# Low parts of the input projections' weights made by an adding DMA

## The chip, the cores and the metric

The kernel runs on one core of one Trainium2 chip. A core has a matrix engine (TensorE, PE in the profile, with its weight loads listed as PEld), three engines for elementwise work (VectorE = DVE, ScalarE = ACT, GpSimd = POOL) and SyncE (SP), which here only issues DMAs. SP, ACT and POOL can issue DMAs; all of them run on the core's 16 DMA engines. The engines work through their own queues of instructions in order, and wait for one another by semaphores. The metric is the device time of one execution in microseconds, the median of several runs.

## The reference

One decoder layer for two groups of tokens with shared weights: a prompt of 1024 positions, and 8 decoding requests of 8 positions (64 in all). The model is 1024 wide.

```python
xn = rmsnorm(x, norm1_g)
proj = xn @ w_in                       # 1024 x 5632: q, k, v, glu_a, glu_b, gate_a, gate_b
q, k, v, glu_a, glu_b, gate_a, gate_b = jnp.split(proj, SPLIT_IDX, axis=-1)
attn = ...                             # sliding window of 128, with sinks
branch_a = attn @ w_o_attn
u = glu_a * jax.nn.sigmoid(glu_b)
c = dwconv_valid(u_ext, conv_b_w, conv_b_bias)      # causal, 31 taps
branch_b = jax.nn.silu(layernorm(c, ln_b_g, ln_b_b)) @ w_pb
merged = jax.nn.sigmoid(gate_a) * branch_a + jax.nn.sigmoid(gate_b) * branch_b
h = x + merged @ w_out
...                                    # a feed-forward block with a short convolution, final norm
```

All tensors are float32. What the edit touches is `w_in`, the weight of the first product.

## The kernel before

**Products in three parts.** TensorE is used with the type float32r, which keeps fewer bits than float32. To keep float32's accuracy, each operand is split in a high part, the value rounded to float32r, and a low part, what the rounding left off. Each product is then three matmuls added up in PSUM (`mm3`, L177 to L181): high weight by high activation (L179), high weight by low activation (L180), low weight by high activation (L181). L181 is the only one that reads a weight's low part as its stationary operand; the two value weights are used the other way round, as moving operands.

**Weights.** All 134 weight tiles lie in one DRAM array `wall`, each 128 partitions by 1024 floats (512 KB), in the order in which they are used (`weight_order`). The first 44 belong to the input projections; `n_in` is 44. `w_load` (L138 to L143) has SP load tile `i` into `wraw`, which has two buffers. `w_split` (L145 to L159) makes the two parts: ScalarE copies the raw tile to `whi` with rounding (L157), VectorE subtracts the rounded tile from the raw one and writes `wlo` (L158). There are two pairs of `whi` and `wlo`, taken in turn, with a tile of the attention pool for one value weight.

**Streams.** `stream` (L183) takes one weight tile and runs it over all 1088 tokens, in chunks of 384, 384 and 320 columns, with 8 slices of 128 rows each: 24 groups of three matmuls. `weight` (L167) is called at the head of each stream and splits the next tile, too: so while stream `i` runs, the parts of tile `i+1` are made, into the pair that stream `i-1` has just let go.

**What runs beside it.** The order of the input streams is written out by hand (`SEQUENCE`). The first four weights run in a stage of their own with the first norm. Then, for each of the eight channel blocks, a `b` and an `a` stream give `u`; `a_done` (L585) has POOL store the convolution's state (`o_cbp`, L587, and `o_cbs`, L588, whose rows are runs of 30 floats) and puts the convolution (`conv`, L405) behind by 1200 steps of priority. The convolution is mostly VectorE's (L417), and its result overwrites `u` and is stored by POOL in two DMAs (`d_c`, L440 and L441). POOL also sets the margins of the next `u` to zero (L558, L559), for which it waits until the stores have read that buffer. Gate streams store their result by POOL (L611), and spills of the attention's output go by POOL, too (L340, L341). Attention units are handed out in small steps between the groups of the streams (`tick`), in two stretches.

The order of the instructions of each engine is set when the kernel is built: among those that are ready by the builder's own simulated time, the one with the best priority goes first. On the chip each engine keeps that order.

Of the kernel before, what the change touches and what calls it, by code (L numbers as in the profile page):

```python
# [6 lines left out]
F32 = mybir.dt.float32  # L7
F32R = mybir.dt.float32r
AF = mybir.ActivationFunctionType
ALU = mybir.AluOpType  # L10
# [35 lines left out]
FIRST = 4  # L46
# [69 lines left out]
class Build:  # L116
# [28 lines left out]
    def w_split(self):  # L145
        i = len(self.w_hl)
        if i < len(self.order):
            r = self.w_raw[i]
            pool, x = self.slot(i)
            th, tl = x if isinstance(x, tuple) else (f"whi{x}", f"wlo{x}")  # L150
            n = 2 if th == tl else 1
            h = self.t(pool, [P, DM], th, F32R, bufs=n)
            l = self.t(pool, [P, DM], tl, F32R, bufs=n)
            m = W_PARTS if i < FIRST else 1
            for x in range(m):
                z = slice(x * DM // m, (x + 1) * DM // m)
                self.nc.scalar.copy(h[:, z], r[:, z])  # L157
                self.nc.vector.tensor_tensor(l[:, z], r[:, z], h[:, z].bitcast(F32), ALU.subtract)  # L158
            self.w_hl.append((h, l))  # L159
# [1216 lines left out]
```

## Time and profile before

| what | value |
|---|---|
| median of 3 runs | 1712.88 us (1711.49 to 1713.6) |
| profiled execution, its own time | 1713.01 us |
| span of the profiled execution | 1711.2 us |
| mean clock granted to TensorE | 0.993 |
| matmul instructions | 11390, busy 98% of the span |
| VectorE, ScalarE, GpSimd busy | 75%, 49%, 14% |

A line of the profile that names a group reads: code line, engine, operation, tile written <- tiles read, shape, count, then busy time and the mean of one in ns, and then how long the engine stood idle just before these instructions and which engine, tile and line ended most of that. A line of a timeline begins with its start and its length in us. The lines of DMA issues give the kilobytes of one and the median time from issue to landing in us. Matmuls overlap in the array, so the listed length of one (about 330 ns) is more than the distance from one to the next.

### The profile page before, as it was taken

Reading aid. Unit: us, or ns where it says so; the run is one execution under the profiler, and the core shown is the slowest. Engines: PE = TensorE matmul, PEld = TensorE weight load, DVE = VectorE, ACT = ScalarE, POOL = GpSimd, SP = SyncE. Lnnn points to the kernel's source line nnn. Section 1 sums busy time; section 2 is a strip of 40 time slices with the busy share of each in tenths; the row PEclk is TensorE's granted clock in tenths of the full one; section 3 lists DMA queues with packets and bytes.
Section 4 is the critical chain, followed back from the end, with each engine's and each line's share of the span. In section 5 each row is a group of like instructions: output and inputs, shape, how many; then the busy total and the mean of one; then the engine's idle time right before and its main releaser. Section 6 shows DMA issues by size and latency. Waiting matters only on the chain.

```text
span 1711.2 us, 29156 instructions
## 1 busy us (share of the span) xinstructions
PE 1681.5 (98%) x11390; PEld 1659.8 (97%) x11390; DVE 1290.3 (75%) x2236; ACT 847.1 (49%) x1718; POOL 242.0 (14%) x430
## 2 busy tenths in 40 slices
PE   9999999999999999999999999999999997999998
PEld 8899999999999999999999999999999996999997
DVE  8999989999579986755447968777777775654437
ACT  7524577733588737963224535444444445211102
POOL 1300112130011111100000432222222210000000
PEclk9999999999999999999999999999999998999999
DMA  5112223232211274544344232222222217643102
GB/s 195 51 53 74 67 63 97 78 125 61 76 44 56 75 259 150 171 159 138 115 132 131 71 110 65 76 77 77 77 77 79 80 62 228 195 121 102 52 1 105
DMA packets 103466, 172.16 MB, mean 101 GB/s; under 512 B 44400, under 2 KB 69376, under 8 KB 103312
## 3 DMA queue, kind: packets, MB, share of 16 engines
q1 hardware_dynamic: 89760, 124.92, 24.2%
q0 software_dynamic: 13424, 45.15, 7.2%
q8 instruction: 89, 1.46, 0.4%
q14 instruction: 49, 0.40, 0.1%
q10 hardware_dynamic: 144, 0.23, 0.0%
HBM read 124.74 MB, written 47.50 MB: 101 GB/s over the span
## 4 chain that ended last, share of the span: by engine, by line
PE 86%; DVE 10%; ACT 2%; DMA 1%; issue 1%; SPq 0%; DVEq 0%; ACTq 0%
PE mm L179 21%; PE mm L180 21%; PE mm L181 21%; PE aux L181 6%; PE aux L180 6%; PE aux L179 6%; DVE c L417 3%; PE aux L303 1%; DVE bt L417 1%; PE aux L315 1%; PE aux L316 1%; PE aux L293 1%; DVE wlo L158 1%; PE aux L294 1%; DVE q L627 1%
## 5 line engine op out<-in xcount | busy, mean ns | idle before, releaser
L179 PE MATMUL mm<-xh,whi 128*128 128x384 f32 (+1 forms) x944 | 314.6, 333 | 0.4 <-ACT xh L217 0.4
L180 PE MATMUL mm<-xl,whi 128*128 128x384 f32 (+1 forms) x944 | 309.2, 328 | 2.5 <-DVE xl L245 1.5
L181 PE MATMUL mm<-xh,wlo 128*128 128x384 f32 (+1 forms) x944 | 308.8, 327 | 0.0
L157 ACT CAST whi<-wraw 128x1024 fp32r<-128x1024 f32 (+1 forms) x91 | 93.6, 1031 | 193.7 <-PE aux L180 104.3
L180 PEld LDWEIGHTS mm<-xl,whi 128*128 128x128 f32 x944 | 177.9, 188 | 5.4 <-DVE xl L245 2.3
L179 PEld LDWEIGHTS mm<-xh,whi 128*128 128x128 f32 x944 | 178.0, 189 | 1.6 <-ACT xh L217 0.7
L181 PEld LDWEIGHTS mm<-xh,wlo 128*128 128x128 f32 x944 | 177.7, 188 | 0.1
L158 DVE TENSOR_TENSOR wlo<-wraw,whi 128x1024 fp32r<-128x1024 f32 (+1 forms) x91 | 108.6, 1197 | 23.5 <-ACT whi L157 23.2
L997 DVE SCALAR_TENSOR_TENSOR acc<-st,fc,acc 128x1104 f32<-128x1104 f32 x88 | 119.8, 1363 | 3.2 <-ACT acc L995 2.5
L179 PE MATMUL mm<-mh,whi 128*128 128x272 f32 x400 | 115.9, 290 | 0.0
L180 PE MATMUL mm<-ml,whi 128*128 128x272 f32 x400 | 115.3, 288 | 0.0
L181 PE MATMUL mm<-mh,wlo 128*128 128x272 f32 x392 | 113.4, 289 | 0.0
L179 PE MATMUL mm<-gh,whi 128*128 128x384 f32 (+3 forms) x264 | 86.4, 327 | 12.5 <-ACT gh L196 12.5
L417 DVE SCALAR_TENSOR_TENSOR bt<-u,consts,bt 128x513 f32<-128x513 f32 x120 | 89.8, 748 | 0.6
L417 DVE SCALAR_TENSOR_TENSOR c<-sm,hsum,c 128x512 f32<-128x512 f32 x120 | 89.6, 746 | 0.7
L181 PE MATMUL mm<-gh,wlo 128*128 128x384 f32 (+3 forms) x264 | 86.5, 328 | 0.0
L179 PE MATMUL aux<-gh,whi 128*128 128x384 f32 (+3 forms) x264 | 86.3, 327 | 0.0
L180 PE MATMUL mm<-gll,whi 128*128 128x384 f32 (+3 forms) x264 | 86.3, 327 | 0.0
L181 PE MATMUL aux<-gh,wlo 128*128 128x384 f32 (+3 forms) x264 | 86.1, 326 | 0.0
L180 PE MATMUL aux<-gll,whi 128*128 128x384 f32 (+3 forms) x264 | 86.0, 326 | 0.0
L417 DVE SCALAR_TENSOR_TENSOR c<-u,consts,c 128x512 f32<-128x512 f32 x112 | 83.5, 746 | 0.4
L180 PEld LDWEIGHTS mm<-ml,whi 128*128 128x128 f32 x400 | 75.4, 188 | 0.0
(362 smaller groups left out, 5166.5 us busy)
## 6 DMA issues: line engine op xcount, KB each, us to landing
wraw<-wall SPq DMA_DIRECT2D x134, 512.0 KB, 3.9
d_g<-acc POOLq DMA_DIRECT2D x22, 552.0 KB, 5.0
gr<-d_g SPq DMA_DIRECT2D x22, 512.0 KB, 5.0
ga<-d_ga SPq DMA_DIRECT2D x8, 544.0 KB, 4.1
gb<-d_gb SPq DMA_DIRECT2D x8, 544.0 KB, 3.6
mar<-d_ma SPq DMA_DIRECT2D x8, 544.0 KB, 5.5
xr<-xT SPq DMA_DIRECT2D x32, 136.0 KB, 2.6
d_h<-H POOLq DMA_DIRECT2D x4, 1088.0 KB, 5.8
```

The costliest lines, as they stand in the source:

```text
L157: self.nc.scalar.copy(h[:, z], r[:, z])
L158: self.nc.vector.tensor_tensor(l[:, z], r[:, z], h[:, z].bitcast(F32), ALU.subtract)
L179: mm(ps, wh, xh, start=first, stop=False, skip_group_check=more)
L180: mm(ps, wh, xl, start=False, stop=False, skip_group_check=more)
L181: mm(ps, wl, xh, start=False, stop=last, skip_group_check=more)
L293: nc.tensor.matmul(ps[:, j, :], q[g][:, h, qs], kd[g][:, keys], start=True, stop=False)
L294: nc.tensor.matmul(ps[:, j, :], q[g][:, h, qs], kl[g][:, keys], start=False, stop=True)
L303: nc.tensor.transpose(ps[:, h * P:(h + 1) * P], pt[:, h, kb * P:(kb + 1) * P], self.ident)
L315: nc.tensor.matmul(av, v, ph, start=kb == kbs[0], stop=False)
L316: nc.tensor.matmul(av, v, pl, start=False, stop=kb == kbs[-1])
L417: mac = lambda o, x, w: nc.vector.scalar_tensor_tensor(o, x, w, o, ALU.mult, ALU.add)
L997: nc.vector.scalar_tensor_tensor(acc, st[:, k:k + AW], fw(f, k), acc, ALU.mult, ALU.add)
```

## The change

For the tiles 4 to 43 of `wall` (`FIRST <= i < n_in`: the input projections' weights, but for the first four) the low part is made in another way. ScalarE makes the rounded tile as before, then reads it back and writes its negative to the tile of the low part. GpSimd then issues a DMA from the raw weight in DRAM to that tile with the operation "add": what lies there, minus the rounded weight, is replaced by its sum with the raw weight. VectorE has no part in it. The raw tile in SBUF is still loaded, and read by the rounding copy alone.

```diff
@@ -151,6 +151,12 @@
             n = 2 if th == tl else 1
             h = self.t(pool, [P, DM], th, F32R, bufs=n)
             l = self.t(pool, [P, DM], tl, F32R, bufs=n)
+            if FIRST <= i < self.n_in:
+                self.nc.scalar.copy(h, r)
+                self.nc.scalar.activation(l, h.bitcast(F32), AF.Identity, scale=-1.0)
+                self.nc.gpsimd.dma_start(l, self.a["wall"][i], accum_op=ALU.add)
+                self.w_hl.append((h, l))
+                return
             m = W_PARTS if i < FIRST else 1
             for x in range(m):
                 z = slice(x * DM // m, (x + 1) * DM // m)
```

All other weights, and the splitting of the activations, stay as they were.

## The prediction

> **What bounds the kernel now.** I read the page's busy table and its chain first, then stage windows of the input projections, then the PE's waits there.
>
> ```profile
> span 1711.2 us, 29156 instructions
> PE 1681.5 (98%) x11390; PEld 1659.8 (97%) x11390; DVE 1290.3 (75%) x2236; ACT 847.1 (49%) x1718; POOL 242.0 (14%) x430
> PE 86%; DVE 10%; ACT 2%; DMA 1%; issue 1%; SPq 0%; DVEq 0%; ACTq 0%
> L181 PE MATMUL mm<-xh,wlo 128*128 128x384 f32 (+1 forms) x944 | 308.8, 327 | 0.0
> ```
>
> The whole span has 30 us without a matmul (1711.2 - 1681.5). L181 is the only matmul that reads the low part as a stationary operand, and its 944 instructions waited 0.0 us. The low part is therefore never late today.
>
> ```profile
> 79.00:110.00 31.00, 31.00 (x187) 31.00 (x188) 30.68 (x45) 10.28 (x19) 4.44 (x8) 1.00 0.26 67
> 110.00:200.00 90.00, 89.71 (x609) 88.92 (x608) 88.69 (x149) 37.26 (x87) 7.90 (x16) 1.00 0.21 62
> 200.00:350.00 150.00, 148.29 (x959) 143.07 (x958) 139.50 (x317) 115.66 (x290) 30.00 (x62) 1.00 0.25 79
> 350.00:455.00 105.00, 105.00 (x643) 104.96 (x642) 94.62 (x143) 36.95 (x73) 17.04 (x34) 1.00 0.30 94
> 455.00:600.00 145.00, 143.99 (x941) 139.38 (x940) 124.48 (x305) 122.15 (x316) 20.71 (x42) 1.00 0.18 56
> 600.00:640.00 40.00, 40.00 (x245) 39.79 (x244) 33.62 (x52) 14.50 (x24) 6.49 (x12) 1.00 0.75 264
> PE aux L315 <- ACT pth L196: 1.7, 2, 1.0
> PE aux L316 <- DVE ptl L197: 0.9, 1, 0.9
> PE mm L180 <- POOL xl L245: 0.6, 1, 0.6
> ```
>
> The columns are stage, length, then PE, PEld, DVE, ACT and POOL busy, the clock, the DMA share and GB/s. In the stage the edit touches, VectorE is busy for 511.6 of 561 us and looks like the bound. PE has only 561 - 558.0 = 3.0 us of gaps, at clock 1.00, and VectorE ended 0.9 us of PE's waits. So 3.0 us is all the stage can give.
>
> **The change part by part.** Forty of the 44 input weights change (44 less FIRST = 4).
>
> ```profile
> L158 DVE TENSOR_TENSOR wlo<-wraw,whi x38: 1210/1220/1230, 82.7 to 637.9; 128x1024 fp32r<-128x1024 f32 x38
> L157 ACT CAST whi<-wraw 128x1024 fp32r<-128x1024 f32 x38 | 40.0, 1053 | 46.9 <-PE mm L180 46.0 <-ACT u L572 0.2
> L577 ACT ACTIVATE u<-u 128x1024 f32<-128x1024 f32 x7 | 7.4, 1064 | 0.1
> L611 POOL DMA_DIRECT2D d_ga<-gt x21 | 11.4, 545 | 50.7 <-ACT gt L608 48.4 <-PE aux L303 1.7 <-ACT av L369 0.6
> ```
>
> *Removed:* 40 subtractions of 1.22 us, 48.8 us of VectorE. They lie beside matmuls, so they are worth at most the 0.9 us of PE's wait on VectorE: I take -0.9.
>
> *Added on ScalarE:* 40 activations, priced by the same-shape ACTIVATE at 1.06 us: 42.6 us, one behind each rounding copy. In the plain stages (37.26 of 90 busy) they hide. In the two attention stages ScalarE stands at 237.8 of 295 us. Some 17 weights fall there, 18 us more, 81% to 87%. It ended 1.7 us of PE's waits on pth; bounds 0 and a doubling, and I take +1.5 because the load is already high. PSUM evacuations and exponentials queue behind each activation.
>
> *Added on GpSimd:* 40 issues; the 545 ns row makes 22 us on an engine busy 86.6 of 561. Hidden as time. The gate stores behind them have no reader before the output projection.
>
> *Moved:* the raw tile is released by the rounding copy instead of the subtraction, so SyncE's next 512 KB load starts a few us sooner, beside the adding DMA. Loads are not late now; the cost falls on the adding DMA. HBM reads grow by 40 x 0.5 MB at a DMA share near 0.2; hidden.
>
> **The new chain.** What matters is the time from a stream's start (when its predecessor's tiles come free) to the next stream's first L181.
>
> ```profile
> 102.96 0.34 PE L179 MATMUL mm<-xh,whi 128*128 128x384 f32 x1
> 114.82 0.34 PE L179 MATMUL mm<-xh,whi 128*128 128x384 f32 x1
> 115.17 0.35 PE L181 MATMUL mm<-xh,wlo 128*128 128x384 f32 x1
> 383.80 1.05 ACT L157 CAST whi<-wraw 128x1024 fp32r<-128x1024 f32 x1 [7.90 <-PE mm L180]
> 395.96 0.35 PE L181 MATMUL mm<-xh,wlo 128*128 128x384 f32 x1
> ```
>
> From 102.96 to 115.17 there are 12.2 us. Rounding copy and activation take 0.05 + 1.05 + 1.06 = 2.2; I add 0.3 for GpSimd to come round to it, an estimate of half an issue. That leaves 9.7 us for the adding DMA, issue to landing. In the attention stages 295 us for some 17 weights is 17.4 each, so about 5 us more.
>
> ```profile
> wraw<-wall SPq DMA_DIRECT2D x39, 512.0 KB, 3.5
> d_c<-u POOLq DMA_DIRECT2D x8, 512.0 KB, 2.9
> o_cbs<-u POOLq DMA_DIRECT2D x8, 120.0 KB, 6.5
> ```
>
> No row shows an adding DMA. A plain load of the size lands in 3.5 us, a plain store in 2.9. The adding one reads raw weight and destination and writes. Lower bound: a plain load, 3.5. Upper: twice a load then a store, 12.8. I take one load and one store end to end, 6.4, nearest in bytes. With 6.4 against 9.7, most of the 40 hide with 3.3 us to spare.
>
> By the Trainium skill, "Collectives: The Full Stack", section "The bandwidth ceiling" (the addition in the DMA engine costs no time of its own; the second source that is read halves the rate), this DMA would land only a little after a load, an estimate; the time would then be that of the rival below in which everything hides. No run here shows an adding DMA yet.
>
> **What comes late.** The spare is used up where GpSimd's queue holds something slow ahead of the adding DMA.
>
> ```profile
> 129.92 0.56 POOL L441 DMA_DIRECT2D d_c<-u  x1 [22.88 <-DVE u L436]
> 133.44 0.54 POOL L440 DMA_DIRECT2D d_c<-u  x1 [2.96 <-DVE u L438]
> 137.16 0.12 POOL L558 MEMSET u<- 128x30 f32 x1 [3.19 <-DMA d_c<-u]
> ...
> 386.56 0.86 POOL L588 DMA_DIRECT2D o_cbs<-u  x1 [0.58 <-issue]
> 387.33 0.62 POOL L440 DMA_DIRECT2D d_c<-u  x1
> 394.83 0.12 POOL L558 MEMSET u<- 128x30 f32 x1 [6.87 <-DMA d_c<-u]
> ```
>
> The store at 133.44 landed 3.7 us later (the memset waits for it). The same store at 387.33, right behind o_cbs with its 120-byte pieces (30 floats each, by the code), landed 7.5 us later. So what follows o_cbs on GpSimd's DMA queue is 3.8 us late. An adding DMA there needs 6.4 + 3.8 = 10.2, and is issued only at 387.4: it lands at 397.6 against 395.96, a stall of 1.6. o_cbs follows each a stream; the plain ones are those after 102.96 and 383.75 (the others have attention's spare): 2 x 1.6 = 3.2 us.
>
> Around 130 the queue waits for the convolution on VectorE (22.88 us) and for its landing.
>
> ```profile
> 127.83 1.05 ACT L157 CAST whi<-wraw 128x1024 fp32r<-128x1024 f32 x1
> 138.89 0.35 PE L181 MATMUL mm<-xh,wlo 128*128 128x384 f32 x1
> 142.47 1.03 ACT L157 CAST whi<-wraw 128x1024 fp32r<-128x1024 f32 x1
> ```
>
> Here the low part is ready to add at 127.83 + 2.11 = 129.9. Ahead of L441 it costs nothing; behind the memset, issue at 137.3 and landing at 143.7, 4.8 us late; behind L440, 140.4, late by 1.5. I take the middle one, 1.5. The copy at 142.47 is 3.9 us into its stream: 144.6 + 6.4 = 151.0 against 150.75 (138.89 and 11.86): 0.3.
>
> **Sum:** -0.9 + 1.5 + 3.2 + 1.5 + 0.3 = +5.6 us, against the profiled run's 1713.0 (the span and 1.8 us around it; 0.1 above the median of 1712.9): 1718.6. The collisions' order on GpSimd can't be read from this trace, and a load beside each adding DMA makes 6.4 optimistic by up to its own 3.5; one us on those five late places adds 4, so I set the forecast at **1720**, own range 1716.5 to 1735.
>
> **Rivals.** *The adding DMA itself is too slow.* From 9.7 us up, each plain stream stalls by the excess. The plain streams show by the copy that starts with each, first and last of a stretch:
>
> ```profile
> 91.15 1.06 ACT L157 CAST whi<-wraw 128x1024 fp32r<-128x1024 f32 x1 [0.44 <-PE mm L180]
> 360.10 1.06 ACT L157 CAST whi<-wraw 128x1024 fp32r<-128x1024 f32 x1 [2.28 <-PE mm L180]
> 431.28 1.05 ACT L157 CAST whi<-wraw 128x1024 fp32r<-128x1024 f32 x1 [2.93 <-PE mm L180]
> 613.13 1.06 ACT L157 CAST whi<-wraw 128x1024 fp32r<-128x1024 f32 x1 [2.32 <-PE mm L180]
> 636.82 1.05 ACT L157 CAST whi<-wraw 128x1024 fp32r<-128x1024 f32 x1 [2.84 <-PE mm L180]
> ```
>
> Seven from 360.10 to 431.28 at 11.86 apiece, three from 613.13 on, and seven from 79 to 162 (one copy ahead of 91.15): 17. At the upper bound of 12.8 that is 17 x 3.1 = 53, and with the forecast's 5.6 on top 1713.0 + 58.6, near 1772. For: no row prices it, and it reads three streams' worth beside a load. Against: 6.4 by the nearest rows. *Everything hides:* landing under 5 us, or GpSimd's queue kept in readiness order. L181 is never late, 1712 to 1714; this is the other side, and the point is an o_cbs-delayed landing below 8.6 us (395.96 - 387.4). For: 12.2 us a stream and a GpSimd idle 85%. *VectorE's relief shows:* the convolutions end sooner, evacuations and splits too, and all 3.0 us of gaps go: 1709 to 1710. Against: VectorE ended 0.9 us of waits only. *The change doesn't relieve anything:* the freed VectorE only idles; that is the second rival's time.
>
> The Trainium skill, "DMA: Bandwidth & Descriptors", Queues, rings and completion order, has each DMA engine consume a ring's descriptors in order, and its section "SWDGE vs HWDGE vs iDMA" gives GpSimd one queue. By that rule the o_cbs wait is real, and the late store at 387.33 agrees (7.5 us against 3.7).
>
> **How the numbers follow.** Forecast 0.36; too slow a DMA 0.32; all hidden 0.22; relief shows 0.10. About 0.2% (3.4 us) is what a measurement can tell from no change. The first two are slower, 0.68; same 0.22; faster 0.10. The range goes down to 1709.5 for most of the relief, and up to 1785 for the slow DMA with the forecast's terms and a little above its bound; the forecast's own range stands above.
>
> **What would show it.** Right: L181 of the changed weights with waits on the DMA of wlo, single digits of them, after o_cbs and after convolution stores; adding DMAs of 5 to 9 us; VectorE some 49 us lighter, ScalarE 43 us heavier; PE's busy sum unchanged. Wrong upward: nearly every plain stream begins with a stall of one size, and landings above 9.7 us. Wrong downward: L181 still at 0.0, landings below 5 us. Also wrong: new PE waits on ScalarE's p or pth of more than 5 us, which would put the cost on the activation.

## The result and the profile after

| | before | changed |
|---|---|---|
| median of 17 runs | 1713.38 us | 1716.53 us |
| ratio, 95% interval | | 1.0018 [1.0011, 1.0025] |
| profiled execution, its span | 1713.01, 1711.2 us | 1715.69, 1713.9 us |

The change costs 3.1 us of 1713 (the profiled pair: 2.7). The interval leaves out 1, so the kernel became slower. The cost is about half of the forecast's 7 and just under the bound of 0.2% that was set for "no change", and 1716.53 lies at the very bottom of the forecast's own range, 1716.5 to 1735. In the changed file the lines after the edit stand six further down: L181 is now L187, L303 is L309, L441 is L447.

The page of the changed kernel, the lines that answer to those of before:

```profile
span 1713.9 us, 29215 instructions
PE 1682.1 (98%) x11390; PEld 1659.5 (97%) x11390; DVE 1245.4 (73%) x2196; ACT 884.3 (52%) x1758; POOL 283.6 (17%) x470
L187 PE MATMUL mm<-xh,wlo 128*128 128x384 f32 (+1 forms) x944 | 309.0, 327 | 3.3 <-DMA wlo<-wall 3.3
wlo<-wall POOLq DMA_DIRECT2D x39, 512.0 KB, 6.6
```

VectorE is 45 us lighter and ScalarE 37 us heavier. PE's busy sum moved by 0.6 us. The adding DMA lands in 6.6 us at the median; the forecast took 6.4. L187 now waits, 3.3 us in all. The stages, in the windows view of the changed kernel, with the same columns as before:

```profile
60.00:79.00 19.00, 17.20 (x103) 16.58 (x102) 18.21 (x29) 12.00 (x25) 9.94 (x13) 1.00 0.27 63
110.00:200.00 90.00, 88.21 (x597) 86.92 (x595) 88.50 (x153) 45.89 (x97) 15.11 (x26) 1.00 0.47 107
200.00:350.00 150.00, 149.29 (x956) 144.64 (x957) 124.57 (x299) 122.90 (x295) 37.64 (x68) 0.99 0.43 109
350.00:455.00 105.00, 103.74 (x634) 103.38 (x632) 77.40 (x123) 43.13 (x78) 31.47 (x42) 1.00 0.59 135
455.00:600.00 145.00, 144.04 (x932) 137.88 (x931) 121.03 (x305) 127.91 (x319) 27.09 (x50) 1.00 0.37 85
```

PE's waits in the changed kernel between 60 and 645 us (sum in us, count, longest):

```profile
PE mm L187 <- DMA wlo<-wall: 3.3, 3, 1.8
PE aux L322 <- DVE ptl L203: 1.6, 2, 1.5
PE aux L321 <- ACT pth L202: 1.5, 5, 0.6
```

The row of before for the first of these stages, which the forecast did not look at:

```profile
60.00:79.00 19.00, 16.94 (x89) 15.41 (x88) 18.88 (x28) 10.06 (x21) 7.95 (x8) 0.91 0.25 82
```

The three waits of the changed kernel's L187, in its PE timeline:

```profile
64.69 0.45 PE L187 MATMUL mm<-xh,wlo 128*128 128x384 f32 x1 [1.79 <-DMA wlo<-wall]
112.70 0.44 PE L187 MATMUL mm<-xh,wlo 128*128 128x384 f32 x1 [0.25 <-DMA wlo<-wall]
443.82 0.44 PE L187 MATMUL mm<-xh,wlo 128*128 128x384 f32 x1 [1.26 <-DMA wlo<-wall]
```

**Where the time went.** A sum of waits doesn't show this well. What does is the start of each stream (its first high-by-high matmul), compared kernel by kernel. Rows of before and of the changed kernel between which the lead changes:

```profile
62.89 0.34 PE L179 MATMUL mm<-xh,whi 128*128 128x384 f32 x1
79.26 0.34 PE L179 MATMUL mm<-xh,whi 128*128 128x384 f32 x1
455.84 0.34 PE L179 MATMUL mm<-xh,whi 128*128 128x384 f32 x1
599.38 0.34 PE L179 MATMUL mm<-xh,whi 128*128 128x384 f32 x1
```

```profile
62.38 0.34 PE L185 MATMUL mm<-xh,whi 128*128 128x384 f32 x1
76.36 0.34 PE L185 MATMUL mm<-xh,whi 128*128 128x384 f32 x1
456.37 0.34 PE L185 MATMUL mm<-xh,whi 128*128 128x384 f32 x1
601.54 0.34 PE L185 MATMUL mm<-xh,whi 128*128 128x384 f32 x1
```

The same subtraction (start in the named kernel less start in before, us) for the changed kernel and for six of the experiments below; the stream itself is named by its start in before. A number that falls from one row to the next is a gain in between, one that rises a loss:

| start in before | what lies ahead of it | changed | first_two | first_two_b | plain_only | act_only | dma_only | plain_copy |
|---|---|---|---|---|---|---|---|---|
| 62.89 | | -0.5 | +1.3 | -0.4 | -0.5 | +1.2 | -0.2 | -0.5 |
| 79.26 | first stage's end | -2.9 | -1.2 | -2.8 | -2.9 | +1.5 | +4.8 | -2.9 |
| 188.71 | plain streams | -2.4 | -1.2 | -2.8 | -2.5 | +2.6 | +5.5 | -2.9 |
| 207.57 | attention, its first stream | -1.3 | +0.4 | -2.8 | -2.8 | +1.6 | +3.8 | -1.1 |
| 360.05 | attention, the rest | -1.0 | +0.3 | -2.8 | -2.7 | +2.3 | +3.7 | -0.8 |
| 455.84 | plain streams | +0.5 | +0.3 | -2.8 | -1.6 | +2.3 | +3.7 | -0.8 |
| 599.38 | attention | +2.2 | +0.3 | -2.8 | -1.6 | +3.4 | +3.6 | +0.8 |
| 648.63 | plain streams | +2.2 | +0.3 | -2.8 | -1.6 | +3.4 | +4.4 | +0.9 |

The changed kernel gains 2.4 us in the first stage, loses 0.5 and 1.5 in plain streams, and 1.4 and 1.6 beside attention. The gain takes back about half of three kinds of loss.

A trace is one execution, and a dip of TensorE's clock can sit in any of its rows. `first_two` and `first_two_b` are the same kernel. The first had lost 1.6 us more at 62.89, with a granted clock of 0.91 over its first 20 us against 1.00 in before, and it loses 1.6 us from 188.71 to 207.57, where its clock reads 0.83. So a step of one or two us in a single trace proves little by itself; what several traces agree on does more.

### The profile page after: what moved, and what is told of

Its sections match the earlier page's. It is cut to its first block, busy times and chain, and to the rows that moved or that the text cites. A ratio compares the mean times of both kernels' runs of the same rounds, so it can differ in the third digit from the quotient of the medians.

```text
span 1713.9 us, 29215 instructions
## 1 busy us (share of the span) xinstructions
PE 1682.1 (98%) x11390; PEld 1659.5 (97%) x11390; DVE 1245.4 (73%) x2196; ACT 884.3 (52%) x1758; POOL 283.6 (17%) x470
## 4 chain that ended last, share of the span: by engine, by line
PE 82%; DVE 9%; ACT 5%; DMA 2%; issue 1%; SPq 0%; POOL 0%; DVEq 0%; ACTq 0%; POOLq 0%
PE mm L185 20%; PE mm L187 20%; PE mm L186 20%; PE aux L187 6%; PE aux L186 6%; PE aux L185 6%; DVE c L423 3%; DVE bt L423 2%; ACT p L276 1%; PE aux L309 1%; DMA wlo<-wall 1%; ACT p L280 1%; PE aux L321 1%; PE aux L322 1%; DVE c L430 1%
## 5 line engine op out<-in xcount | busy, mean ns | idle before, releaser
L187 PE MATMUL mm<-xh,wlo 128*128 128x384 f32 (+1 forms) x944 | 309.0, 327 | 3.3 <-DMA wlo<-wall 3.3
L187 PEld LDWEIGHTS mm<-xh,wlo 128*128 128x128 f32 x944 | 177.5, 188 | 4.4 <-DMA wlo<-wall 4.3
L163 ACT CAST whi<-wraw 128x1024 fp32r<-128x1024 f32 (+1 forms) x52 | 52.5, 1014 | 146.3 <-PE aux L186 103.7
L187 PE MATMUL mm<-mh,wlo 128*128 128x272 f32 x392 | 113.4, 289 | 0.0
L187 PE MATMUL mm<-gh,wlo 128*128 128x384 f32 (+3 forms) x264 | 86.5, 328 | 0.0
L187 PE MATMUL aux<-gh,wlo 128*128 128x384 f32 (+3 forms) x264 | 86.0, 326 | 0.0
L185 PEld LDWEIGHTS mm<-mh,whi 128*128 128x128 f32 x400 | 75.3, 188 | 0.0
```

The source lines that it names most:

```text
L185: mm(ps, wh, xh, start=first, stop=False, skip_group_check=more)
L187: mm(ps, wl, xh, start=False, stop=last, skip_group_check=more)
```

## The experiments

The theory after this reading: VectorE's relief pays in the first stage alone; adding DMAs are late where something holds them up; ScalarE's extra activations cost beside attention. The rivals: that the first stage's gain is only a dip of TensorE's clock that fell elsewhere, that ScalarE's load is the whole cost, or that late landings are.

**Weights 4 and 5 alone**

```diff
-            if FIRST <= i < self.n_in:
+            if FIRST <= i < FIRST + 2:
```

> Only the low parts of weights 4 and 5 are made by the adding DMA; the other 38 go by VectorE as before. Theory (the changed kernel gains in the first stage, where VectorE is the late engine, and loses afterwards): the start of the stream after weight 4, 79.26 us before and 76.36 us after, stays near 76.4, nothing is lost later, so the time is 2 to 3 us under the kernel before (about 1710.5). PE still waits some 1.8 us for the second of the two DMAs. Rival (the earlier start is only a dip of TensorE's clock that fell elsewhere in the profiled run): no difference from before, within 1 us.

Measured: 1710.96 us against 1713.62, ratio 0.9986 [0.9978, 0.9995]. Two of the 40 edited weights make the kernel faster than before. The PE's wait for the second low part was 0.3 us, not the 1.8 expected. The same kernel was measured again later:

> The version with weights 4 and 5 alone once more, on another occasion. Theory (VectorE's chain in the first stage is shorter by two subtractions): 2 to 3 us under before again, interval below 1. Rival (the first measurement was the clock's doing): the interval holds 1.

Measured: 1710.44 against 1712.74, ratio 0.9989 [0.9980, 0.9998]. PE waited 0.9 us for a low part in this trace. The rival fell: the gain came back. Where it comes from is seen in the timeline of VectorE, in before:

```profile
61.36 1.21 DVE L158 TENSOR_TENSOR wlo<-wraw,whi 128x1024 fp32r<-128x1024 f32 x1
62.49 1.37 DVE L245 TENSOR_TENSOR xl<-xr,xh 128x384 fp32r<-128x384 f32 x1
63.78 1.21 DVE L158 TENSOR_TENSOR wlo<-wraw,whi 128x1024 fp32r<-128x1024 f32 x1
64.92 2.14 DVE L249 RECIPROCAL rstd<-rstd 128x320 f32<-128x320 f32 x1
```

and in the timeline of PE, in before:

```profile
72.64 0.42 PE L180 MATMUL mm<-xl,whi 128*128 128x320 f32 x1 [1.09 <-DVE xl L245]
74.19 0.41 PE L180 MATMUL mm<-xl,whi 128*128 128x320 f32 x1 [0.40 <-DVE xl L245]
78.86 0.42 PE L180 MATMUL mm<-xl,whi 128*128 128x320 f32 x1 [0.57 <-POOL xl L245]
```

and on VectorE of the changed kernel:

```profile
60.82 0.55 DVE L251 TENSOR_TENSOR xl<-xr,xh 128x384 fp32r<-128x384 f32 x1
61.97 2.15 DVE L255 RECIPROCAL rstd<-rstd 128x320 f32<-128x320 f32 x1 [0.60 <-ACT rstd L254]
```

Two subtractions of 1.21 us stood in VectorE's queue ahead of the reciprocal that the last chunk's norm needs. Without them it starts at 61.97 instead of 64.92. The stage ends with the last piece of that chunk's low part, which GpSimd makes, in before and in the changed kernel:

```profile
77.11 1.69 POOL L245 TENSOR_TENSOR xl<-xr,xh 128x320 fp32r<-128x320 f32 x1 [0.92 <-ACT xh L243]
```

```profile
74.20 1.71 POOL L251 TENSOR_TENSOR xl<-xr,xh 128x320 fp32r<-128x320 f32 x1 [0.92 <-ACT xh L249]
```

In before it is done at 78.80, and the next stream starts at 79.26; in the changed kernel these are 75.91 and 76.36. From the start at 62.89 on, the stage is 2.4 us shorter in the changed kernel and in both traces of weights 4 and 5 alone. That is the time of the two subtractions, whether PE waited 1.8, 0.3 or 0.9 us for a low part on the way.

**Weight 5 alone**

```diff
-            if FIRST <= i < self.n_in:
+            if i == FIRST + 1:
```

> Only weight 5, the second of the two, by the adding DMA. Theory: the first stage gains one subtraction of 1.2 us instead of two, and the wait on wlo near 65 us, if it is weight 4's, goes: 1 to 2.5 us under before. Rival (the gain needs both): no gain.

Measured: 1711.10 against 1712.74, ratio 0.9993 [0.9985, 1.0002]. The interval holds 1, so the time settles nothing. In its trace the first stage ended 2.3 us earlier than in before, nearly as much as with both, and PE did not wait for wlo.

**All but weights 4 and 5**

```diff
-            if FIRST <= i < self.n_in:
+            if FIRST + 2 <= i < self.n_in:
```

> Weights 4 and 5 go by VectorE as before, the other 38 by the adding DMA. Theory: the first stage is as before and all the losses after it stay: slower than before by 5 us (3.1 measured for all 40 and 2 to 3 no longer gained), less the 1.8 us that PE waited for weight 4 or 5, so +3 to +5. Rival (the cost lies in the first stage's late DMA): no slower than before, +0 to +1.

Measured: 1717.33 against 1713.62, ratio 1.0023 [1.0014, 1.0032], so +3.7: the losses without the gain. -2.7 and +3.7 make +1.0, not the +3.1 of all 40. The difference of 2.1 us is not explained; each of the three numbers has an interval of 1.2 to 1.5 us to either side.

**ScalarE's part alone**

```diff
                 self.nc.scalar.activation(l, h.bitcast(F32), AF.Identity, scale=-1.0)
-                self.nc.gpsimd.dma_start(l, self.a["wall"][i], accum_op=ALU.add)
+                self.nc.vector.tensor_tensor(l, r, h.bitcast(F32), ALU.subtract)
```

> ScalarE writes the negative as in the changed kernel, but then VectorE overwrites it with the difference, as before; there is no adding DMA. This is ScalarE's 42 us alone, with VectorE's 49 us back. Theory (the DMA's rare late landings cost 3.3 us, ScalarE's load costs PE some 1.5 us more waiting in the attention stages): +1 to +3 us on before, no wait on wlo. Rival (ScalarE's load costs all of it): +4 us or more, the same waits on pth and p as in the changed kernel and more. Rival (ScalarE's load is free): within 0.5 us.

Measured: 1715.15 against 1713.62, ratio 1.0009 [1.0000, 1.0018]: +1.5, no wait on wlo. In the table of starts it loses 1.1 us from 455.84 to 599.38, and 0.7 from 207.57 to 360.05.

**The DMA without ScalarE's part**

```diff
-                self.nc.scalar.activation(l, h.bitcast(F32), AF.Identity, scale=-1.0)
+                self.nc.vector.tensor_scalar(l, h.bitcast(F32), -1.0, None, ALU.mult)
```

> VectorE, not ScalarE, writes the negative; then the DMA adds. ScalarE has its load of before, VectorE nearly its load of before. Theory: the chain to the DMA starts later, because VectorE came to the subtraction 1 to 5 us after the rounding copy, so with a landing of 6.6 us against 9.7 us of room more low parts are late than the three of the changed kernel: PE waits on wlo 5 to 15 us, time +4 to +15. Rival (the cost is ScalarE's load): faster than the changed kernel, within 1 us of before.

Measured: 1718.28 against 1713.62, ratio 1.0028 [1.0016, 1.0039]. The waits on wlo are as large as expected, but they are not spread out. PE's waits from 40 to 655 us in this kernel, and behind them the longest one in PE's timeline:

```profile
PE mm L187 <- DMA wlo<-wall: 7.9, 3, 7.2
```

```profile
70.36 0.69 PE L187 MATMUL mm<-xh,wlo 128*128 128x384 f32 x1 [7.20 <-DMA wlo<-wall]
```

One wait of 7.2 us in the first stage, where VectorE comes late to the negative. From 360.05 to 599.38 this kernel loses nothing (+3.7 to +3.6), with the same DMAs in flight beside attention. So neither the DMAs nor their traffic cost anything there.

**Attention's weights left to VectorE**

```diff
-            if FIRST <= i < self.n_in:
+            if FIRST <= i < 15 or 25 <= i < 33 or 42 <= i < self.n_in:
```

> The adding DMA for the 21 weights that are split in the plain stretches (4 to 14, 25 to 32, 42 and 43); the 19 that are split beside attention work go by VectorE as before. Theory (beside attention ScalarE's extra activations cost some 2 us; in the plain stretches only late landings cost): the stretch from 456 to 600 us costs nothing any more, the waits on wlo near 65, 113 and 444 us stay, the time is 2 us under the changed kernel, within 1 us of before (1713 to 1714.5). Rival (the loss in the attention stretches comes from the traffic of the adding DMAs or from the shifted order): the same, since the DMAs there are gone, too; against this stands the run in which VectorE wrote the negatives. Rival (the loss is all from late landings): no better than the changed kernel.

Measured: 1712.86 against 1712.74, ratio 1.0001 [0.9992, 1.0010]. Of the three waits on wlo, the one near 113 us did not come. The 1.6 us from 455.84 to 599.38 are gone (-1.6 to -1.6), and so is the 1.4 us of the first attention stretch. For the second stretch this places the loss on the activations: `act_only` (1.1 us) and `plain_copy` (1.6) lose there, too, and `dma_only`, with the DMAs but without the activations, does not. The loss is no single wait: between these two starts the waits view gives PE 0.9 us on pth in the changed kernel and 1.0 in before.

For the first stretch the activations are shown for a small part only. Of the changed kernel's 1.4 us, 1.1 lie from 188.71 to 207.57, where its clock reads 0.83. `act_only` loses nothing there, and `first_two`, with no changed weight near, loses 1.6. The other 0.3 us, from 207.57 to 360.05, is lost by `act_only` (0.7) and `plain_copy` (0.3) as well, and not by `first_two`, `first_two_b` and `dma_only`.

**The margins cleared by VectorE**

```diff
-            nc.gpsimd.memset(u[:, 0:HIST], 0.0)
-            nc.gpsimd.memset(u[:, HIST + SEQ:PW], 0.0)
+            nc.vector.memset(u[:, 0:HIST], 0.0)
+            nc.vector.memset(u[:, HIST + SEQ:PW], 0.0)
```

> The changed kernel, but VectorE instead of GpSimd clears the margins of the next u, so no adding DMA stands behind an instruction that waits for a store of the convolution to land. Theory (GpSimd's queue made that low part late): the wait of 1.26 us on wlo near 444 us is gone, the one near 65 us stays, the time is about 1 us under the changed kernel unless VectorE's own wait costs as much. Rival (the adding DMA itself was slow there): the wait stays.

The reason for it is this stretch of the changed kernel's GpSimd:

```profile
430.56 0.56 POOL L447 DMA_DIRECT2D d_c<-u  x1 [3.65 <-DVE u L442]
431.12 0.54 POOL L617 DMA_DIRECT2D d_gb<-gt  x1
432.33 0.54 POOL L446 DMA_DIRECT2D d_c<-u  x1 [0.67 <-issue]
432.86 0.54 POOL L617 DMA_DIRECT2D d_gb<-gt  x1
437.14 0.12 POOL L564 MEMSET u<- 128x30 f32 x1 [3.74 <-DMA d_c<-u]
437.19 0.10 POOL L565 MEMSET u<- 128x2 f32 x1
437.88 0.89 POOL L157 DMA_DIRECT2D wlo<-wall  x1 [0.58 <-issue]
```

ScalarE had written the negative by 432.6, but GpSimd waited 3.74 us for a store to land before it could clear the margins, and only then issued the adding DMA: landing 5.9 us later, PE waiting until 443.8. Measured: 1718.28 against 1713.46, ratio 1.0031 [1.0020, 1.0041]. The wait near 444 us is gone, as the theory had it. But now VectorE waits for those stores, 11 us in three waits. One of them is 4.6 us near 176 us, in a stretch (160 to 202 us) in which VectorE had no wait in the changed kernel, and PE has a new wait of 2.8 us on p near 199 us. Another new wait, of 1.0 us at the LayerNorm's sums, is not shown to be VectorE's doing: it comes in the next run, too (1.7 us), where GpSimd clears the margins. The wait moved to a worse engine.

**The small pieces sent by SyncE**

```diff
-            nc.gpsimd.dma_start(a["o_cbs"][i], us[:, :, NT:])
+            nc.sync.dma_start(a["o_cbs"][i], us[:, :, NT:])
```

> The changed kernel, but SyncE issues o_cbs, so its 120-byte pieces don't go down GpSimd's queue ahead of an adding DMA. Theory (what follows o_cbs on that queue lands some 3 us later): the adding DMAs after an a stream land in about 6 us where they took 8.4 to 9.0, and the wait of 0.25 us near 113 us is gone. Rival (the pieces load the DMA engines, from whichever queue they come): still 8 to 9 us. Time of the whole within 1 us of the changed kernel by either.

Issues near 103 us, first the changed kernel, then this one (columns as in the lines of DMA issues):

```profile
wlo<-wall POOLq DMA_DIRECT2D x1, 512.0 KB, 9.0
o_cbs<-u POOLq DMA_DIRECT2D x1, 120.0 KB, 6.7
```

```profile
wlo<-wall POOLq DMA_DIRECT2D x1, 512.0 KB, 9.7
o_cbs<-u SPq DMA_DIRECT2D x1, 120.0 KB, 7.2
```

The theory fell: with o_cbs in another engine's queue the adding DMA beside it still takes 9.7 us. Over the whole kernel the adding DMAs issued while o_cbs is on its way take 7.9 to 9.0 us in the changed kernel and 7.9 to 9.7 us here, where undisturbed ones take some 5.5. So the small pieces delay the DMA beside them from whichever queue they come. One run, 1718.2 us; its time tells no more than that nothing was gained.

**A plain DMA in the place of the adding one**

```diff
-                self.nc.gpsimd.dma_start(l, self.a["wall"][i], accum_op=ALU.add)
+                self.nc.gpsimd.dma_start(l, self.a["wall"][i])
```

> The changed kernel with a plain DMA in the place of the adding one, of the same size, from the same queue: the low part is then the raw weight, so the difference is left out of the result. This prices the addition. Theory of the forecast (the adding DMA also reads its destination): the plain one lands in 3.5 to 4.5 us where the adding one took 6.6. Rival (the queue and the type are what costs, not the addition): 5.5 to 6.6 us as before. Time: 0 to 3 us under the changed kernel, the waits on wlo gone or nearly.

The rows of the low part's DMA, of the changed kernel and of this one:

```profile
L157 POOL DMA_DIRECT2D wlo<-wall x39: 842/876/1034, 52.3 to 629.8; - x39
DMA to landing us min/median/max: 5.4/6.6/9.0
```

```profile
L157 POOL DMA_DIRECT2D wlo<-wall x39: 528/542/683, 52.3 to 628.5; - x39
DMA to landing us min/median/max: 3.9/4.7/8.4
```

Adding costs 1.9 us of landing (6.6 less 4.7) and 0.33 us of GpSimd's time per issue. Without it PE never waits on wlo, and the run took 1713.6 us. In the table of starts it keeps the first stage's gain, loses nothing in the plain streams, and still loses 1.6 us in the second attention stretch: ScalarE's part again.

**The addition twice**

```diff
                 self.nc.gpsimd.dma_start(l, self.a["wall"][i], accum_op=ALU.add)
+                self.nc.gpsimd.dma_start(l, self.a["wall"][i], accum_op=ALU.add)
```

> The changed kernel with a second adding DMA behind each first, on the same tile (the result then holds the raw weight once too often). The second waits for the first, so the low part comes 6.6 us + some 0.5 later: from the activation's end 13 to 14 us against 9.7 of room in a plain stream. Theory (9.7 us of room, 17 plain streams): each plain stream begins with a wait on wlo of 3 to 5 us, 60 to 90 us in all, the attention stages add some; time 1780 to 1830. Rival (the room is larger than worked out): under 1750.

PE's waits on wlo in this run (its second DMA moved the matmul lines by one more):

```profile
PE mm L188 <- DMA wlo<-wall: 66.0, 16, 11.6
PE mm L187 <- DMA wlo<-wall: 3.4, 1, 3.4
```

Measured: 1804.2 us, with 69 us of waits on wlo and a granted clock of 0.973 instead of 0.993 over the run. So one adding DMA fits into the room of 9.7 us and two don't. The waits came in 17 pieces of 0.3 to 11.6 us, many at every second stream, rather than in one of 3 to 5 us at each plain one.

## Why the prediction was right, and where it was not

*The direction and the chain were right.* One adding DMA fits into the 9.7 us that a plain stream leaves (6.6 measured, 6.4 taken), and two don't (1804 us). L187 waited three times in the whole kernel, which the forecast had as "single digits". VectorE became 45 us lighter and ScalarE 37 heavier, where 49 and 43 were worked out, and behind the first stage no row shows a gain from VectorE's relief.

*The size was not.* Two terms were far off, and both made the sum too large: the gain in the first stage was 1.5 us larger than taken, the loss to o_cbs 2.7 us smaller. A third term had the right size at the wrong place. That the sum still came within about a factor of two is partly luck.

*VectorE's relief: -0.9 taken, -2.4 measured.* The cause is a window. The stage table began at 79 us, but weights 4 and 5 are split at 61 to 65 us, in the first norm's stage, where VectorE is busy 18.88 of 19 us and PE had 2.06 us of gaps. So "3.0 us is all the stage can give" was said of a stage from which the part with the gain was left out. Runs with only those two weights gain 2.7 and 2.3 us.

*ScalarE's load: +1.5 taken, +1.9 measured* (0.3 and 1.6 beside attention), with 1.1 us more near 200 us that are not shown to be the activations' doing (they go with a clock dip, below). The sign and the place were right. The size was drawn from the waits view, which doesn't show this loss; the starts of streams do.

*o_cbs: +3.2 taken, +0.5 measured.* An adding DMA near one did land late: 9.0 us against some 5.5 for undisturbed ones, where 10.2 was worked out. Near 113 us that cost a wait of 0.25 and 0.5 us of lead; near 395 us the adding DMA took 8.4 us and cost nothing. The mechanism was wrong in one step: the delay was put down to the order in GpSimd's queue, but from SyncE the pieces delay the adding DMA as much (9.7 us). The Trainium skill has a rule for this in "DMA: Bandwidth & Descriptors", section "Issuing engines are not separate DMA queues": DMAs from all issuing engines run on the same 16 engines and interleave. The run agrees (9.7 us).

*The convolution's store: +1.5 taken, +1.5 measured, at another place.* Near 139 us it cost nothing; near 444 us the order "behind the memset" came about. Which collision it would be couldn't be read from the trace of before, as the forecast said, so that the two sizes agree is luck.

*The late rounding copy (+0.3)* cost nothing, and the allowance of 1.4 on the top of the sum was not needed either. That allowance doesn't follow from its own words: the sum lists four late places, not five, and 4 us on 1718.6 would have made 1722.6. The terms that were too small and those too large left 2.7 of the 7 forecast in the profiled pair.

*The rivals.* The one in which the DMA is too slow needed a landing over 9.7 us and got 6.6. The one in which everything hides fell with the three waits. The one in which VectorE's relief shows was half true, and it was given too little. The Trainium skill's account of an addition in the DMA engine ("Collectives: The Full Stack", "The bandwidth ceiling") has it cost only the second read, which halves the rate. That the adding DMA would land "only a little after a load" does not follow from a halved rate, and it did not: 6.6 us against 3.5 for a load. Against a plain DMA from the same queue it took 6.6 us for 4.7; this is less than twice, and no run here separates the second read from the addition.

## What to carry to other kernels

When an edit relieves a busy engine, look for the place where the bound engine waits for it, and begin the table of stages where the first edited instruction runs, not where the stage seems to begin. Here no gain shows from 38 of the 40 relieved subtractions, and the other two were worth 2.4 us; applying the change to these two alone gives 0.9986 [0.9978, 0.9995] and 0.9989 [0.9980, 0.9998] of the time before. A DMA in the chain of a double-buffered tile costs nothing as long as it lands within the stream. What made it late here was what its issuing engine waited for ahead of it (1.5 us near 444 us) and, less, the small pieces beside it (0.5 us near 113 us).

## What the runs showed of the hardware

TensorE's granted clock dips for a moment near short waits, but not near each of them. 10 us windows of before, of the changed kernel and of `first_two`, in this order:

```profile
70.00:80.00 10.00, 7.94 (x38) 6.74 (x37) 9.88 (x17) 5.40 (x14) 5.93 (x7) 0.83 0.04 16
200.00:210.00 10.00, 8.35 (x56) 7.61 (x55) 10.00 (x23) 6.43 (x18) 2.30 (x5) 1.00 0.10 41
```

```profile
200.00:210.00 10.00, 9.49 (x54) 9.22 (x55) 9.28 (x27) 6.23 (x17) 0.74 (x2) 0.83 0.16 48
```

```profile
200.00:210.00 10.00, 8.46 (x46) 8.00 (x47) 9.13 (x22) 5.71 (x16) 1.87 (x4) 0.83 0.10 41
```

A clock of 0.83 over 10 us costs about 1.7 us where PE is the bound (0.17 of 10, an estimate). Before has this dip at its three waits near 75 us. It is no part of the first stage's gain, since PE still had to wait for GpSimd's last piece behind it (0.57 us at 78.86). Near 200 us the changed kernel has the dip with 2.0 us of waits on pth and ptl. Before and `first_two` have the same three waits there, some 1.9 us on p, pth and ptl in each; before keeps 1.00 and `first_two` reads 0.83. So what decides it stays open, and 1.1 us of the changed kernel's loss can't be put down to the edit. The spread between runs of one kernel goes with the clock: the 17 runs of the changed kernel have spans of 1712.3 us at a mean clock of 0.995 and of 1715.7 to 1717.3 at 0.991.
